# A Strassen-form feed-forward kernel: the next block's chain tiles are loaded into other buffers two products earlier, some transposes stand one product later, and the entry to the second feed-forward is reordered

## Chip, cores and metric

The kernel runs on one core of a Trainium2 chip. The metric is the time of one execution on the device in microseconds (us); several executions are given by their median. The page of the profile and the trace are of one further execution, taken by the hardware profiler.

## The reference, cut to what matters

One layer with the same weights for 256 context tokens and 256 latent tokens, everything in float32, model width 2048, feed-forward width 5632:

```
def half_step_ffn(x, mod, i, g, w_up, w_down):
    h = adaln(x, g, mod, i)                     # RMS norm, scale, shift
    a, b = jnp.split(h @ w_up, 2, axis=-1)
    return x + 0.5 * mod[:, i + 2, None, :] * ((jax.nn.silu(a) * b) @ w_down)

xl = half_step_ffn(xl, mod_l, 0, ...)           # first feed-forward, latent
xc = half_step_ffn(xc, mod_c, 0, ...)           # and context tokens
...                                             # mixing: attention and mLSTM heads
xl = half_step_ffn(xl, mod_l, 6, ...)           # second feed-forward, latent tokens only
return rms_norm(xl, g_final)
```

The modulation vectors (`mod_l`, `mod_c`) are products of a condition vector with a 2048 x 18432 matrix. They are computed beside the feed-forwards.

## The kernel before

**Products.** A float32 product is made of three TensorE products in fp32r. Both operands are split into a high part (ScalarE rounds a copy, `ringhi` on L140 or L170) and a low part (VectorE subtracts, `ringlo` on L141 or L171); high x high, high x low and low x high are added up in PSUM. Weights stream from HBM in tiles of 128 x 2048 float32 (1 MB). Every weight tile is split when it is used, into a ring of four half-tile slots, so that the split of one tile runs while TensorE works on the tile before.

**Blocks.** The hidden width is cut into 11 blocks of 512. In the up-projections of most blocks a 2 x 2 block product is done with seven products instead of eight. `quad(n)` does this for block n. Its table `order` has one row for each of the seven products (`a11`, `a12`, `n1`, `s4`, `s2`, `s3`, `a22`, named by their token form), and each is done in two tiles, q = 0 and 1. So a block has 14 places, 0 to 13: place 2m + q is tile q of product m. The columns of a row are the token form, where the weight tile comes from, the PSUM bank, whether it starts fresh, what is issued behind the split, and what is done with the result.

**The chain.** Four of the seven products take their weight tiles from two buffers, `chain_[0]` and `chain_[1]`: they are loaded with the first weight form (places 0 and 1), and after each use GpSimd issues a DMA that adds the next difference of weights to them in place (`accum`, L784). Places 2 and 3 take plain tiles from the pool `raw` (three buffers), places 6 and 7 take two more raw tiles (`ra`) to which an accumulating DMA adds another form for places 10 and 11. The function `again` behind place 12 + q loads `chain_[q]` for the next block, since before this the tile is still read. These loads stand on the queue of the SP engine, in order, together with all others: `chain` loads on L817 (first feed-forward), L1159 (its down-projection) and L2113 (second feed-forward), plain tiles on L952, `ra` tiles on L947.

**First feed-forward.** `quad(1)` to `quad(10)` do the up-projection; each product has 24 matmuls of 128 x 512 for a tile. Results are combined (`ca`, L896 and L897), transposed on TensorE (L893) and sent to HBM. The loads and vector work of the modulation products (`sraw`, L263 and L292) are woven in. `pair(p)` then does the down-projection of two hidden blocks at a time in the same seven products, with its own `again`.

**Second feed-forward.** It has 256 tokens only. Its entry does the first hidden block in plain products (L1955 to L1962: Silu, multiply, `split_hid`). Then two streams are interleaved: `quads()` (seven blocks in the seven-product form, 12 matmuls for each tile) and `units()` (three blocks in plain form and all down-projections, 24 matmuls for each tile). `places()` says how many units follow each place. `turned()` transposes a finished hidden tile on TensorE (L2049) once at least three tiles have passed since it was made (`turn[0][-1] + 3 > tiles[0]` holds it back), and splits it into `hid2h` and `hid2l` (L2052, L2054). The token forms (`token_forms`, L2000, L2001 and L2005) are made at the entry. PSUM is handed from one set of pools to another there (`banks.close()`), so the first matmul of the second feed-forward proper waits for the last reader of the old banks, the multiply on L1961.

A scheduler orders the instructions of each engine. `tc.keep_in_program_order(ins)` pins an instruction to where it was written.

Of the kernel before, what the change touches and what calls it, by code (L numbers as in the profile page):

```python
# [9 lines left out]
F32 = mybir.dt.float32  # L10
# [4 lines left out]
ALU = mybir.AluOpType  # L15
# [4 lines left out]
P = 128  # L20
# [41 lines left out]
def tile_layer(ctx: ExitStack, tc: tile.TileContext, I: dict, out: bass.AP):  # L62
# [53 lines left out]
    cbT = vecs[:, 272:288]  # L116

    def raw_tile(n=2048):
        t = wp.tile([P, 2048], F32, tag="raw", name="raw", bufs=3)
        return t if n == 2048 else t[:, :n]  # L120
# [16 lines left out]
    def split_whole(raw):  # L137

        hi, lo = ring(2)
        nc.scalar.activation(hi, raw, AF.Copy)  # L140
        nc.vector.tensor_tensor(lo, raw, hi.bitcast(F32), op=ALU.subtract)  # L141
        return lambda w: (hi[:, w], lo[:, w])

    def load_whole(src):
# [640 lines left out]
    with pool(name="f1u", bufs=1) as f1u:  # L785
# [30 lines left out]
        def first_chain(n, c):  # L816
            nc.sync.dma_start(chain_[c], part(n, 0, c))  # L817
# [81 lines left out]
        def quad(n, after=lambda step: None):  # L899
# [36 lines left out]
            def chained(ab, c):  # L936
                return lambda q: accum(chain_[q], part(n, ab, c + q))

            def again(q):
                if n + 1 < NB:  # L940
                    first_chain(n + 1, q)
                else:
                    nc.sync.dma_start(chain_[q], I["w_dn1"][0, 2 * q])

            def loaded(q):
                ra[q] = raw_tile()
                nc.sync.dma_start(ra[q], part(n, 1, 2 + q))  # L947
                return ra[q]

            def plain(q):  # L950
# [155 lines left out]
    def pair(p):  # L1106
# [44 lines left out]

        def loaded(m, cb):
            raw = raw_tile()
            nc.sync.dma_start(raw, w(m, cb))
            return raw

        def again(c):
            if p + 1 < NP:
                nc.sync.dma_start(chain_[c], I["w_dn1"][2 * p + 2, 2 * c])  # L1159

        def b22(c):
            ra[c] = loaded(1, 2 * c + 1)
            return ra[c]
# [7 lines left out]
            ("a11", held, X, True, lambda c: accum(chain_[c], w(0, 2 * c + 1)), c11x),  # L1171
            ("a12", lambda c: loaded(1, 2 * c), Z, True, None, c11z),
# [3 lines left out]
            ("s3", lambda c: ra[c], X, False, None, x3),  # L1176
            ("a22", held, Y, True, again, c21),
        )
# [32 lines left out]
    for p in range(NP):  # L1211
        pair(p)

    def block_products(b, wt, t):
# [707 lines left out]
    with f2x:  # L1922
# [28 lines left out]
        for f in range(NPRE, FB):  # L1951
            pab = []
            for ab in range(2):
                wt = load_split(I["w_up2"][f, ab])
                b = bank()[:, :T]  # L1955
                for k in range(KT):
                    mm3(b, *wt(slice(k * P, (k + 1) * P)), h2hi[:, k, :T], h2lo[:, k, :T], k == 0, k == KT - 1)
                pab.append(b)
            sa = sab_tile()[:, :T]
            nc.scalar.activation(sa, pab[0], AF.Silu)  # L1960
            nc.vector.tensor_tensor(sa, sa, pab[1], op=ALU.mult)  # L1961
            split_hid(hids[0], f, sa)  # L1962
        hscm.__exit__(None, None, None)
# [30 lines left out]

        def ra_tile():
            return f2b.tile([P, 2048], F32, tag="ra", name="ra")

        def token_forms():
# [8 lines left out]

            def difference(v, x, y):
                (h1, l1), (h2, l2) = f32(x), f32(y)
                sub(v, h1, h2)  # L2010
                nc.vector.tensor_tensor(v, v, l1, op=ALU.add)
                sub(v, v, l2)
# [6 lines left out]
            v, w = (acc2[:, t, 1024:].rearrange("p (k c) -> p k c", k=8) for t in range(2))  # L2019
            difference(v, a22, a21)  # L2020
            put(n1, v)
# [15 lines left out]
        def turned():  # L2037

            if not turn or turn[0][-1] + 3 > tiles[0]:
                return  # L2040
# [27 lines left out]
        def quad(n):  # L2068
# [53 lines left out]
            def plain(q):  # L2122
# [290 lines left out]
```

## Time and profile before

| | |
|---|---|
| median of 3 runs | 2645.22 us (2639.3 to 2656.01) |
| profiled execution, own time | 2644.05 us |
| its span, first to last instruction | 2642.3 us |
| granted TensorE clock, mean | 0.996 |
| TensorE (PE) busy | 2595.9 us, 98% |
| weight loads (PEld) busy | 2148.3 us, 81% |
| VectorE (DVE) busy | 2181.9 us, 83% |
| ScalarE (ACT) busy | 1345.2 us, 51% |
| first feed-forward, up | about 150 to 960 us |
| first feed-forward, down | about 960 to 1330 us |
| mixing | about 1330 to 1930 us |
| second feed-forward | about 1930 to 2643 us |

Busy time is the union of an engine's instructions. Idle time of an engine is given with the event that ended it. A number such as 1.79 in square brackets behind an instruction is how long its engine stood idle just before.

### The profile page before, as it was taken

The page shows a single profiled execution, that of the slowest core. Times are in us where ns is not written, and L with a number is a line of the kernel's source. Part 1 is how long each engine was busy: PE and PEld are TensorE (multiplying, and loading weights), DVE is VectorE, ACT ScalarE, POOL GpSimd, SP SyncE. Part 2 cuts the span into 40 slices and gives each one's busy share as a digit, 9 for nine tenths or more (in the row PEclk, how much of TensorE's full clock was granted, in tenths as well). Part 3 has the DMA queues.
Part 4 walks back from the last instruction along what each step waited for, and adds up shares of the span by engine and source line. Part 5 has one row for each costly group of instructions (what it writes and reads, how often), then busy time and mean ns, then how long its engine had stood idle before and what let it go on. Part 6 is the DMA issues. An engine that isn't in the chain of part 4 may idle for free. (4 is left out here: it accounts for less than half of the span.)

```text
span 2642.3 us, 33359 instructions
## 1 busy us (share of the span) xinstructions
PE 2595.9 (98%) x12670; PEld 2148.3 (81%) x12670; DVE 2181.9 (83%) x2817; ACT 1345.2 (51%) x1547; POOL 210.7 (8%) x265
## 2 busy tenths in 40 slices
PE   8999999999999999999999999999999999999998
PEld 5787888888888878888889888877898888888887
DVE  6687888878878778888886979798598888887888
ACT  4354444544444455444454346346476555555554
POOL 0000001100000100010110000111000000000001
PEclk9999999999999999999999999999999999999999
DMA  9979999999999988889985867574568999889886
GB/s 376 343 229 259 257 283 269 271 285 280 271 280 268 276 230 237 221 208 230 231 244 215 315 227 246 207 271 159 175 253 262 294 273 295 259 271 307 285 244 188
DMA packets 136800, 679.94 MB, mean 257 GB/s; under 512 B 14392, under 2 KB 24376, under 8 KB 75840
## 3 DMA queue, kind: packets, MB, share of 16 engines
q1 hardware_dynamic: 108384, 496.92, 50.4%
q0 software_dynamic: 27968, 180.37, 34.8%
q8 instruction: 99, 1.62, 0.2%
q10 hardware_dynamic: 288, 0.52, 0.1%
q14 instruction: 61, 0.50, 0.1%
HBM read 658.82 MB, written 18.94 MB: 256 GB/s over the span
## 5 line engine op out<-in xcount | busy, mean ns | idle before, releaser
L170 ACT ACTIVATE ringhi<-raw 128x1024 fp32r<-128x1024 f32 (+4 forms) x363 | 370.6, 1025 | 429.0 <-PE mm L194 286.3
L171 DVE TENSOR_TENSOR ringlo<-raw,ringhi 128x1024 fp32r<-128x1024 f32 (+3 forms) x340 | 405.7, 1203 | 125.6 <-ACT ringhi L170 110.8
L192 PE MATMUL mm<-ringhi,hhi 128*128 128x512 f32 (+3 forms) x1024 | 391.0, 384 | 0.6 <-ACT ringhi L170 0.6
L193 PE MATMUL mm<-ringlo,hhi 128*128 128x512 f32 (+3 forms) x1024 | 387.5, 378 | 1.0 <-DVE ringlo L171 0.9
L194 PE MATMUL mm<-ringhi,hlo 128*128 128x512 f32 (+3 forms) x1024 | 387.2, 378 | 0.0
L170 ACT ACTIVATE ringhi<-chain 128x1024 fp32r<-128x1024 f32 x240 | 253.1, 1059 | 239.9 <-PE mm L194 143.3
L171 DVE TENSOR_TENSOR ringlo<-chain,ringhi 128x1024 fp32r<-128x1024 f32 x240 | 290.0, 1221 | 69.8 <-ACT ringhi L170 69.0
L263 DVE SCALAR_TENSOR_TENSOR junk<-sraw,cBh 128x1024 fp8e5<-128x1024 f32 x192 | 234.4, 1221 | 44.9 <-DMA sraw<-in_w_mt 42.6
L193 PEld LDWEIGHTS mm<-ringlo,hhi 128*128 128x128 f32 x1024 | 192.7, 188 | 33.5 <-DVE ringlo L171 2.6
L194 PEld LDWEIGHTS mm<-ringhi,hlo 128*128 128x128 f32 x1024 | 192.5, 188 | 33.4
L192 PEld LDWEIGHTS mm<-ringhi,hhi 128*128 128x128 f32 x1024 | 192.5, 188 | 31.7 <-ACT ringhi L170 0.8
L140 ACT ACTIVATE ringhi<-raw 128x2048 fp32r<-128x2048 f32 x78 | 149.7, 1920 | 129.3 <-PE mm L155 75.8
L141 DVE TENSOR_TENSOR ringlo<-raw,ringhi 128x2048 fp32r<-128x2048 f32 x78 | 178.6, 2289 | 39.1 <-ACT ringhi L140 37.6
L141 DVE TENSOR_TENSOR ringlo<-chain,ringhi 128x2048 fp32r<-128x2048 f32 x56 | 128.2, 2288 | 27.6 <-ACT ringhi L140 27.5
L140 ACT ACTIVATE ringhi<-chain 128x2048 fp32r<-128x2048 f32 x56 | 107.5, 1919 | 81.1 <-PE mm L155 26.9
L154 PE MATMUL mm<-ringhi,hid2h 128*128 128x512 f32 x320 | 124.7, 390 | 0.0
L155 PE MATMUL mm<-ringhi,hid2l 128*128 128x512 f32 x320 | 124.5, 389 | 0.0
L784 POOL DMA_DIRECT2D chain<-in_w_up1b x60 | 52.4, 873 | 651.5 <-DVE ringlo L171 543.1
L263 DVE SCALAR_TENSOR_TENSOR sr<-sr,cBl 128x1024 f32<-128x1024 f32 x72 | 87.1, 1215 | 7.2 <-DMA sr<-in_w_mt 7.1
L194 PE MATMUL mm<-hhi,ringlo 128*128 128x512 f32 (+1 forms) x256 | 87.9, 343 | 4.5 <-DVE ringlo L171 4.4
L192 PE MATMUL mm<-hhi,ringhi 128*128 128x512 f32 (+1 forms) x256 | 88.7, 347 | 0.0
L193 PE MATMUL mm<-hlo,ringhi 128*128 128x512 f32 (+1 forms) x256 | 87.0, 340 | 0.0
(513 smaller groups left out, 5940.2 us busy)
## 6 DMA issues: line engine op xcount, KB each, us to landing
raw<-in_w_dn SPq DMA_DIRECT2D x70, 1024.0 KB, 7.5
sraw<-in_w_mt SPq DMA_DIRECT2D x128, 512.0 KB, 7.7
chain<-in_w_up1b POOLq DMA_DIRECT2D x60, 1024.0 KB, 10.9
raw<-in_w_up1b SPq DMA_DIRECT2D x40, 1024.0 KB, 9.3
raw<-in_w_up2b SPq DMA_DIRECT2D x38, 1024.0 KB, 7.6
sr<-in_w_mt SPq DMA_DIRECT2D x69, 512.0 KB, 5.5
mraw<-in_w_m SPq DMA_DIRECT2D x32, 1024.0 KB, 9.2
chain<-in_w_dn POOLq DMA_DIRECT2D x30, 1024.0 KB, 8.5
```

The costliest lines, as they stand in the source:

```text
L140: nc.scalar.activation(hi, raw, AF.Copy)
L141: nc.vector.tensor_tensor(lo, raw, hi.bitcast(F32), op=ALU.subtract)
L154: nc.tensor.matmul(out_ap, sh, mh, start=first, stop=False, skip_group_check=True)
L155: nc.tensor.matmul(out_ap, sl, mh, start=False, stop=False, skip_group_check=True)
L170: nc.scalar.activation(hi, src, AF.Copy)
L171: vector[0].tensor_tensor(lo, src, hi.bitcast(F32), op=ALU.subtract)
L192: tensor[0].matmul(out_ap, sh, mh, start=first, stop=False, skip_group_check=skip)
L193: tensor[0].matmul(out_ap, sh, ml, start=False, stop=False, skip_group_check=skip)
L194: tensor[0].matmul(out_ap, sl, mh, start=False, stop=last, skip_group_check=skip)
L263: ins = nc.vector.scalar_tensor_tensor(junk() if junk else raw, raw, 1.0, cB[s], op0=ALU.mult, op1=ALU.mult, accum_out=mT[:, i, s, kt, h : ...
L784: accum = lambda dst, src: nc.gpsimd.dma_start(dst, src, accum_op=ALU.add)
```

## The change

**Buffers.** In the first feed-forward the three raw tiles become named buffers in a list `free`. `take()` removes the first of the list, `give(t)` puts one back at the end. The chain's two tiles join the rotation: while block n is in place 8 (`s2`, q = 0) the first chain tile of block n + 1 is loaded into a free buffer, in place 10 (`s3`, q = 0) the second (`ahead`); `passed` makes it the chain's tile in places 12 and 13 and gives the old one back. `pair` does the same at `s3` (`next_first`). In the second feed-forward the chain's tiles and the `ra` tiles of the third form (`s4`, `s3`) change places from block to block: the next chain tile is loaded into `ra[q]` behind the split of place 10 + q, and the old chain tile serves as `ra[q]` of the next block.

**Transposes.** A tile of the second token half that carries a minus sign (`turn[0][3] < 0 and turn[0][1]`) is transposed once four tiles have passed, not three.

**Entry of the second feed-forward.** The split of the last hidden tile of block 0 (`split_hid` for f = 3) is written behind the first unit. The first split of a weight tile there, and the first subtraction of the token forms, are pinned in program order.

```
+    free = [wp.tile([P, 2048], F32, name=f"raw{i}", bufs=1) for i in range(3)]
+    def take():
+        return free.pop(0)
+    def give(t):
+        free.append(t)
     def raw_tile(n=2048):
-        t = wp.tile([P, 2048], F32, tag="raw", name="raw", bufs=3)
+        t = take()
+        give(t)
...
# split_whole
+        if in_order:
+            in_order.pop()
+            tc.keep_in_program_order(low)
...
# quad, first feed-forward
-            def again(q):
-                if n + 1 < NB:
-                    first_chain(n + 1, q)
-                else:
-                    nc.sync.dma_start(chain_[q], I["w_dn1"][0, 2 * q])
+            def ahead(q):
+                following[q] = take()
+                nc.sync.dma_start(following[q], part(n + 1, 0, q) if n + 1 < NB else I["w_dn1"][0, 2 * q])
+            def after_s2(q):
+                chained(0, 2)(q)
+                if not q:
+                    ahead(0)
+            def after_s3(q):
+                give(ra[q])
+                if not q:
+                    ahead(1)
+            def passed(q):
+                give(chain_[q])
+                chain_[q] = following[q]
...
-                (s2, held, X, False, chained(0, 2), c12),
-                (s3, lambda q: ra[q], X, False, None, c22),
-                (a22, held, Y, True, again, c21),
+                (s2, held, X, False, after_s2, c12),
+                (s3, lambda q: ra[q], X, False, after_s3, c22),
+                (a22, held, Y, True, passed, c21),
...
# pair, down-projection of the first feed-forward
+        def next_first(c):
             if p + 1 < NP:
-                nc.sync.dma_start(chain_[c], I["w_dn1"][2 * p + 2, 2 * c])
+                following[c] = take()
+                nc.sync.dma_start(following[c], I["w_dn1"][2 * p + 2, 2 * c])
+            give(ra[c])
...
# entry of the second feed-forward
-            split_hid(hids[0], f, sa)
+            if f < FB - 1:
+                split_hid(hids[0], f, sa)
+        in_order.append(True)
...
+                if in_turn:
+                    tc.keep_in_program_order(ins)
...
-            if not turn or turn[0][-1] + 3 > tiles[0]:
+            if not turn or turn[0][-1] + 3 + (turn[0][3] < 0 and turn[0][1]) > tiles[0]:
...
# quad, second feed-forward
-            def again(q):
+            def ahead(q):
                 after = [x for x in QUADS if x > n]
                 if after:
-                    nc.sync.dma_start(chain_[q], part(after[0], 0, q))
+                    nc.sync.dma_start(ra[q], part(after[0], 0, q))
+            def passed(q):
+                spare[q], chain_[q] = chain_[q], ra[q]
             def loaded(q):
-                ra[q] = ra_tile()
+                ra[q] = spare[q]
...
-                (s3, lambda q: ra[q], "X", False, None, c22),
-                (a22, held, "Y", True, again, c21),
+                (s3, lambda q: ra[q], "X", False, ahead, c22),
+                (a22, held, "Y", True, passed, c21),
...
# units, behind the first one
+                if sa is not None:
+                    split_hid(hids[0], FB - 1, sa)
+                    sa = None
```

**The SP queue in the first feed-forward**, toward the end of a block of the up-projection. Before, L952 loads plain tile 1 of the next block, L947 `ra` tile 0 of the next block, and L817 the chain's two tiles of the next block.

```order
L952 DMA raw_3149<-in_w_up1b 128x2048
L947 DMA raw_3259<-in_w_up1b 128x2048
L292 DMA sraw_2871<-in_w_mt 128x1024
L884 DMA hid3_1399<-stg_2894 128x512
L817 DMA chain0_1416<-in_w_up1b 128x2048
L292 DMA sraw_2915<-in_w_mt 128x1024
L292 DMA sraw_2956<-in_w_mt 128x1024
L884 DMA hid3_1399<-stg_2975 128x512
L817 DMA chain1_1417<-in_w_up1b 128x2048
```

In the changed kernel L958 is `ahead` (a chain tile of the next block), L981 a plain tile and L976 an `ra` tile; the buffer's name no longer tells the role.

```order
L958 DMA raw0_84<-in_w_up1b 128x2048
L981 DMA raw1_85<-in_w_up1b 128x2048
L307 DMA sraw_2847<-in_w_mt 128x1024
L899 DMA hid3_1386<-stg_2871 128x512
L981 DMA chain0_1403<-in_w_up1b 128x2048
L307 DMA sraw_2892<-in_w_mt 128x1024
L307 DMA sraw_2932<-in_w_mt 128x1024
L899 DMA hid3_1386<-stg_2951 128x512
L976 DMA chain1_1404<-in_w_up1b 128x2048
```

The sequence of transfers is the same in both, four weight tiles in the same four slots. Only the roles moved: the slots that loaded plain 1, `ra` 0, chain 0 and chain 1 now load chain 1, plain 0, plain 1 and `ra` 0. Chain 0 stands in the slot of a weight tile still further ahead, where plain 0 was.

**TensorE in the second feed-forward**, at the end of a block. Before, the transposes of the block's last hidden tile (L2049) stand behind a down-projection tile and ahead of the first product of the next block (`X`).

```order
L155 MATMUL mm<-ringhi,hid2l 128x512
L160 MATMUL mm<-ringlo,hid2h 128x512 x8
L2049 MATMUL tr<-ident,ca 128x128 x4
L154 MATMUL X<-ringhi,h2hi 128x512
L155 MATMUL X<-ringhi,h2lo 128x512
```

In the changed kernel the same transposes are L2090, behind the first tile of `X` (L169, L170, L175).

```order
L169 MATMUL X<-ringhi,h2hi 128x512
L170 MATMUL X<-ringhi,h2lo 128x512
L175 MATMUL X<-ringlo,h2hi 128x512 x4
L2090 MATMUL tr<-ident,ca 128x128 x4
L169 MATMUL X<-ringhi,h2hi 128x512
```

They moved back by one tile of 12 matmuls. This is so at the end of six of the seven blocks. In two of the six, two groups of transposes of a plain block follow and move back too.

**VectorE at the entry of the second feed-forward.** Before, rows on L2000 and L2011 are parts of the token forms, L141 is the low part of the first weight tile and L1961 the multiply that reads the last of the old PSUM banks.

```order
L2000 TENSOR_TENSOR acc_14841<-h2hi 128x1024
L1945 SCALAR_TENSOR_TENSOR sab<-sab,shift 128x256
L2011 TENSOR_TENSOR acc_14841<-acc_14841,h2lo 128x1024
L1933 TENSOR_TENSOR hid2l<-sab,hid2h 128x256
L2000 TENSOR_TENSOR acc_14841<-acc_14841,h2lo 128x1024 x2
L141 TENSOR_TENSOR ringlo<-raw,ringhi 128x2048
L1961 TENSOR_TENSOR sab<-sab,mm 128x256
```

In the changed kernel the multiply is L1999, the low part L151, and L2039 and L2052 are the token forms.

```order
L2039 TENSOR_TENSOR acc_14688<-acc_14688,h2lo 128x1024
L1983 SCALAR_TENSOR_TENSOR sab<-sab,shift 128x256
L2039 TENSOR_TENSOR s3f<-acc_14688,s3f 128x1024
L1971 TENSOR_TENSOR hid2l<-sab,hid2h 128x256
L1999 TENSOR_TENSOR sab<-sab,mm 128x256
L151 TENSOR_TENSOR ringlo<-raw_86,ringhi 128x2048
L1971 TENSOR_TENSOR hid2l<-sab,hid2h 128x256
L2039 TENSOR_TENSOR acc_14688<-h2hi 128x1024
L151 TENSOR_TENSOR ringlo<-raw_84,ringhi 128x2048
L2052 TENSOR_TENSOR acc_14688<-acc_14688,h2lo 128x1024
L2039 TENSOR_TENSOR acc_14688<-acc_14688,h2lo 128x1024
```

The multiply now stands ahead of the first low part. One of the two differences of the token forms (three operations) moved from ahead of it to behind it, between the low parts, and the low part of `s3f` moved ahead of it.

More of the change, by code (lines that the diff above doesn't have):

```diff
@@ L140, in split_whole @@
         nc.scalar.activation(hi, raw, AF.Copy)
-        nc.vector.tensor_tensor(lo, raw, hi.bitcast(F32), op=ALU.subtract)
+        low = nc.vector.tensor_tensor(lo, raw, hi.bitcast(F32), op=ALU.subtract)
+        if in_order:
+            in_order.pop()
+            tc.keep_in_program_order(low)
         return lambda w: (hi[:, w], lo[:, w])
+    in_order = []
     def load_whole(src):
@@ L1150, in c21, with loaded, passed @@
             through_gate(2 * s + 1, 2 * c)
-        def loaded(m, cb):
-            raw = raw_tile()
+        def loaded(m, cb, raw):
             nc.sync.dma_start(raw, w(m, cb))
             return raw
-        def again(c):
+        following = {}
+        def next_first(c):
             if p + 1 < NP:
-                nc.sync.dma_start(chain_[c], I["w_dn1"][2 * p + 2, 2 * c])
+                following[c] = take()
+                nc.sync.dma_start(following[c], I["w_dn1"][2 * p + 2, 2 * c])
+            give(ra[c])
+        def passed(c):
+            give(chain_[c])
+            chain_[c] = following.get(c)
         def b22(c):
-            ra[c] = loaded(1, 2 * c + 1)
+            ra[c] = loaded(1, 2 * c + 1, take())
             return ra[c]
@@ L1212, in tile_layer @@
         pair(p)
+    free[:] = [t for t in free if any(t is x for x in lasting)]
+    assert len(free) == len(lasting)
     def block_products(b, wt, t):
@@ L1993, in tile_layer @@
         n1, s4, s2, s3 = ([x[:, 0], x[:, 1]] for x in (forms2[g] for g in ("n1", "s4", "s2", "s3")))
-        def ra_tile():
-            return f2b.tile([P, 2048], F32, tag="ra", name="ra")
+        spare = [f2b.tile([P, 2048], F32, name=f"ra{q}", bufs=1) for q in range(2)]
         def token_forms():
@@ L2019, in token_forms @@
             v, w = (acc2[:, t, 1024:].rearrange("p (k c) -> p k c", k=8) for t in range(2))
[L2020 removed]
+            difference(v, a22, a21, True)
             put(n1, v)
```

14 lines of the change are left out of this document (8 added, 6 removed).

## The prediction

> **What bounds the kernel now.** First the page: how much of the span TensorE is busy.
>
> ```profile
> PE 2595.9 (98%) x12670; PEld 2148.3 (81%) x12670; DVE 2181.9 (83%) x2817; ACT 1345.2 (51%) x1547; POOL 210.7 (8%) x265
> ```
>
> TensorE's matmuls fill 98%; no other engine is near. An idle share of 2% may still sit in one stage, so the busy times by stage come next: the first feed-forward up and down, the entry of the second, and the rest of the second.
>
> ```profile
> core 0: us, PE busy (x) PEld busy (x) DVE busy (x) ACT busy (x) POOL busy (x), PEclk, DMA share, GB/s
> 150.00:960.00 810.00, 804.80 (x3609) 663.05 (x3609) 675.23 (x844) 401.04 (x463) 71.54 (x82) 1.00 0.98 272
> 960.00:1330.00 370.00, 367.80 (x1615) 303.65 (x1614) 311.24 (x341) 182.52 (x184) 40.63 (x47) 1.00 0.89 226
> 1982.00:2010.00 28.00, 27.64 (x122) 22.91 (x123) 23.95 (x18) 15.11 (x12) 1.85 (x2) 1.00 0.84 272
> 2010.00:2602.00 592.00, 588.22 (x2631) 485.82 (x2630) 500.84 (x374) 336.93 (x230) 37.19 (x43) 1.00 0.89 274
> ```
>
> In the stages that the change touches TensorE is idle for 810 − 804.80 = 5.2, 2.2, 0.4 and 3.8 us; 1.8 us just ahead of 1982 come to it (below). That is **13.4 us** in all, at full clock, and no edit removes or adds a matmul. So the sum can't be large; the question is which of these gaps go, and whether a new one opens.
>
> Is "busy" at the floor? One run of matmuls in the timeline of TensorE, first and last of thirteen:
>
> ```profile
> 789.76 0.39 PE L194 MATMUL mm<-ringhi,hlo 128*128 128x512 f32 x1
> 792.48 0.39 PE L194 MATMUL mm<-ringhi,hlo 128*128 128x512 f32 x1
> 794.66 0.63 PE L893 MATMUL tr<-ident,ca 128*128 128x128 f32 x4 [1.79 <-DVE ca L897]
> ```
>
> Twelve steps take 2.72 us, 0.227 each; a tile of 24 matmuls takes 5.44 us, one of 12 takes 2.72. The third row is a gap of the kind sought: transposes that wait 1.79 us for a VectorE result.
>
> [...]
>
> **The chain tiles in the first feed-forward.** Who waited for the early loads of L817 (the view of that line):
>
> ```profile
>   ACT ringhi L170: 12.7, 6
> DMA to landing us min/median/max: 4.7/6.5/7.9
> ```
>
> ScalarE stood 12.7 us in six waits. To see what of it reaches TensorE, the two places in time order; SP's issue, ScalarE's wait, VectorE's result, TensorE (for the second, TensorE is above).
>
> ```profile
> 392.81 0.33 SPq L817 DMA_DIRECT2D chain<-in_w_up1b  x1
> 399.88 2.01 ACT L170 ACTIVATE ringhi<-chain 128x1024 fp32r<-128x1024 f32 x2 [1.27 <-DMA chain<-in_w_up1b]
> 404.32 0.50 PE L193 MATMUL mm<-ringlo,hhi 128*128 128x512 f32 x1 [0.90 <-DVE ringlo L171]
> ...
> 783.54 0.34 SPq L817 DMA_DIRECT2D chain<-in_w_up1b  x1
> 791.59 1.06 ACT L170 ACTIVATE ringhi<-chain 128x1024 fp32r<-128x1024 f32 x1 [5.73 <-DMA chain<-in_w_up1b]
> 792.56 0.61 ACT L932 ACTIVATE ca<-ca 128x512 f32<-128x512 f32 x1
> 793.83 0.68 DVE L897 TENSOR_TENSOR ca<-ca,cy 128x512 f32<-128x512 f32 x1
> ```
>
> The load lands 7 to 8 us after its issue; the split of it blocks ScalarE's queue, the Silu behind it (L932) comes late, then VectorE, then TensorE: **0.9 us at 404 and 1.79 us at 794**. The other four waits are swallowed by the ring. The remaining 5.2 − 2.7 = 2.5 us in this stage follow other events (modulation tiles, a store of hidden tiles), and I leave them.
>
> What is late next, once the chain is early? The slots of the SP queue stay, so I set them against the need, ScalarE's first split of each tile in the block that begins at 470.
>
> ```profile
> 452.37 0.33 SPq L952 DMA_DIRECT2D raw<-in_w_up1b  x1
> 457.25 0.33 SPq L947 DMA_DIRECT2D raw<-in_w_up1b  x1
> 462.82 0.33 SPq L817 DMA_DIRECT2D chain<-in_w_up1b  x1
> ...
> 470.52 1.06 ACT L170 ACTIVATE ringhi<-chain 128x1024 fp32r<-128x1024 f32 x1 [0.35 <-PE mm L194]
> 475.98 1.06 ACT L170 ACTIVATE ringhi<-chain 128x1024 fp32r<-128x1024 f32 x1 [3.01 <-PE mm L194]
> 481.89 1.06 ACT L170 ACTIVATE ringhi<-raw 128x1024 fp32r<-128x1024 f32 x1 [0.80 <-PE mm L194]
> 487.35 1.06 ACT L170 ACTIVATE ringhi<-raw 128x1024 fp32r<-128x1024 f32 x1 [0.81 <-PE mm L194]
> ...
> DMA to landing us min/median/max: 7.1/9.3/11.5
> DMA to landing us min/median/max: 6.6/9.3/14.9
> ```
>
> The last two rows are the landing times of the loads on L952 and L947. Before, chain 0 leaves at 462.82 and is needed at 470.52: 7.7 us for a load of 6.5 to 7.9. After, chain 1 leaves at 452.37 for 475.98 (23.6 us), plain 0 at 457.25 for 481.89 (24.6), plain 1 at 462.82 for 487.35 (24.5). The longest load of these lines takes 14.9, so the smallest spare time goes from about zero to some 9 us. Number and size of transfers are the same, hence no more load on the DMA engines. Term: **−2.7 us**, bounds 0 (VectorE, 83% busy here, is late anyway) and −5.2 (all gaps of the stage go).
>
> In `pair` the same swap applies; TensorE's gaps of 2.2 us there mostly follow the stage's first tiles, whose loads are not moved in it. Term 0, bounds 0 and −2.2.
>
> **The end of a block in the second feed-forward.** TensorE's waits there, and one case in time order, ScalarE, VectorE, TensorE:
>
> ```profile
> PE tr L2049 <- DVE ca L2071: 3.8, 4, 1.3
> ...
> 2166.38 1.92 ACT L140 ACTIVATE ringhi<-chain 128x2048 fp32r<-128x2048 f32 x1 [3.41 <-DMA chain<-in_w_up2b]
> 2170.53 0.69 DVE L2071 TENSOR_TENSOR ca<-ca,cy 128x512 f32<-128x512 f32 x1
> 2171.36 0.63 PE L2049 MATMUL tr<-ident,ca 128*128 128x128 f32 x4 [1.29 <-DVE ca L2071]
> ```
>
> Four waits, 3.8 us, the longest 1.3: the whole idle time of the stage. The chain tile again holds back a Silu, and through it the multiply on L2071. The change acts twice: the chain is loaded two places earlier, and the transposes stand 12 matmuls, 2.72 us, later, more than the longest wait. Either is enough for this case. Term: **−3.8 us**, bounds 0 and −3.8.
>
> The transposes that move pull their followers along, ScalarE's and VectorE's splits into `hid2h` and `hid2l`:
>
> ```profile
> 2172.03 0.60 ACT L2052 ACTIVATE hid2h<-tr 128x512 fp32r<-128x512 f32 x1 [1.29 <-PE tr L2049]
> 2174.53 0.68 DVE L2054 SCALAR_TENSOR_TENSOR hid2l<-tr,hid2h 128x512 fp32r<-128x512 f32 x1
> ```
>
> From transposes to the end of `hid2l` it is 2175.21 − 2171.36 = 3.9 us. In the new order 36 matmuls (12 of `X`, 24 of `Y`) stand between the transposes and the first reader of the new hidden tile: 8.2 us. So this is covered, with some 4 us to spare.
>
> **The entry.** VectorE and TensorE around 1980:
>
> ```profile
> 1979.60 2.28 DVE L141 TENSOR_TENSOR ringlo<-raw,ringhi 128x2048 fp32r<-128x2048 f32 x1
> 1981.81 0.41 DVE L1961 TENSOR_TENSOR sab<-sab,mm 128x256 f32<-128x256 f32 x1
> 2001.35 1.22 DVE L2000 TENSOR_TENSOR s4f<-acc,s4f 128x1024 fp32r<-128x1024 f32 x1
> ...
> 1980.26 0.28 PE L194 MATMUL mm<-h2hi,ringlo 128*128 128x256 f32 x1
> 1982.36 0.47 PE L154 MATMUL mm<-ringhi,h2hi 128*128 128x512 f32 x1 [1.82 <-DVE sab L1961]
> ```
>
> The multiply that frees the old banks could begin at 1980.54, when the last matmul ends, but VectorE has just begun a 2.28 us low part and reaches it at 1981.81. With the multiply ahead, TensorE can start at about 1980.6 + 0.41 + 0.1 = 1981.1, 1.2 us earlier. The low part then runs from 1981.0 to 1983.3; a unit reads it after 16 matmuls on the high part, at 1981.1 + 3.6 = 1984.7. In exchange three token operations (1.22 us each, the row of L2000) move behind and one ahead, 2 x 1.22 = 2.4 us more for VectorE by 2010, and TensorE comes 1.2 us sooner: 3.6 us against VectorE's idle 28.00 − 23.95 = 4.05 us. Just covered. Term: **−1.2 us**, bounds +2.3 (the cover fails and one low part is late) and −1.8 (no wait left).
>
> **Sum.** −2.7 − 3.8 − 1.2 = −7.7 us on the profiled execution's own 2644.05 (its span, 2642.3, and 1.75 around it): 2636.3. That execution lies 1.2 us below the median of the runs, 2645.22; I give 2636. The best bound is −13.4 (2630.7). A measurement of this kernel can tell about 1%, 26 us, from no change, so this forecast, 0.3%, lies within it.
>
> **Rivals.**
>
> - **The waits move on to another engine (0.17).** VectorE is 83 to 85% busy in these stages, and a tile made ready early only queues ahead of the same work; each gap comes back somewhere else. Against it: both cases show ScalarE stopped by a landing, with VectorE idle behind it. It would give 2643.
> - **Slower: the hidden forms come late (0.06).** The moved transposes put `hid2h` behind another 1.92 us high part and `hid2l` behind another 2.29 us low part. If the sum passes the 8.2 us, the down-projection waits. The point is 4.3 us more than today's 3.9; the price, one low part of 2.29 us past it at each of six places, +13.7, and the 3.8 still gone: 2644.05 − 7.7 + 13.7 = 2650.
> - **All gaps close (0.04):** −13.4, 2630.7.
> - **Slower still: a load misses its slot (0.02).** If loads took over 24.6 us, each of ten blocks would lose the excess; at 3 us each 2666. The longest seen is 14.9.
> - **The swap has no effect (0.02),** since SP sends the same sequence: 2644. The rows of the order speak against it.
> - **TensorE has hidden room (0.01).** The later chain loads, L1159 and L2113, were waited for by ScalarE as well:
>
> ```profile
>   ACT ringhi L170: 5.4, 2
>   ACT ringhi L140: 13.9, 6
> ```
>
> If all its waits came back whole in the end, 12.7 + 5.4 + 13.9 = 32.0 us, it would be 2612. [...]
>
> **Numbers.** The forecast has 0.68. The range 2628 to 2648 takes in forecast, no effect and all gaps closed, with the scatter of single runs (2639.3 to 2656.01 before). Faster by over 1% needs 26 us where 13.4 are idle: 0.02. Slower by over 1%: 0.03, part of the missed slots and what I don't see. Within 1%: 0.95.
>
> **What would show it.** No wait of ScalarE for the new chain loads in the first feed-forward (12.7 to about 0); no TensorE gap at transposes in either feed-forward for a late Silu; the wait for L2071's successor (L2112) at 0; TensorE's gap at the entry 0.6 us instead of 1.82; idle time of TensorE in 2010 to 2602 under 1 us. I am wrong if the waits for `hid2h` appear ahead of the down-projection, if low parts are late in the first two units and products of the second feed-forward, or if TensorE's idle time stays at 46 us.

## The result, and the profile after

| | before | after |
|---|---|---|
| median | 2645.22 us (13 runs, 2638.21 to 2656.01) | 2635.06 us (13 runs, 2628.88 to 2639.77) |
| profiled execution, own time | 2644.05 us | 2633.05 us |

The medians lie 10.2 us apart. The ratio is 0.9958, 95% interval 0.9946 to 0.997, so the changed kernel takes between 8 and 14 us less. The forecast of 2636 lies 0.9 us above the median after. The change is small and not zero.

TensorE's share of the span, from the page of the changed kernel, and then the four stages as they were shown of before, with the same columns:

```profile
PE 2591.7 (98%) x12670; PEld 2145.9 (82%) x12670; DVE 2180.7 (83%) x2817; ACT 1345.4 (51%) x1547; POOL 210.2 (8%) x265
...
150.00:960.00 810.00, 808.53 (x3635) 666.49 (x3633) 680.71 (x849) 406.73 (x469) 71.39 (x82) 1.00 0.98 273
960.00:1330.00 370.00, 366.56 (x1616) 303.01 (x1615) 311.31 (x344) 180.11 (x180) 42.65 (x49) 1.00 0.90 226
1982.00:2010.00 28.00, 28.00 (x125) 23.21 (x124) 27.40 (x20) 18.27 (x15) 1.85 (x2) 1.00 0.90 261
2010.00:2602.00 592.00, 592.00 (x2650) 489.69 (x2649) 505.75 (x380) 334.64 (x228) 40.46 (x46) 1.00 0.89 277
```

The share is 98% in both, so the page alone would show nothing. By stage TensorE's idle time went from 5.2 to 1.5 us, from 2.2 to 3.4 (the down-projection of the first feed-forward, a little worse), from 0.4 to 0 and from 3.8 to 0. The gap ahead of 1982 is in the waits of TensorE from 1960 to 2602, which have a single row left; the waiters for the multiply ahead of the transposes (L2112, L2071 before) follow it:

```profile
PE mm L169 <- DVE sab L1999: 0.7, 1, 0.7
...
  PEld tr L2090: 0.3, 1
```

1.82 us became 0.7. Together the idle time of these stages fell from 13.4 to 5.6 us: 7.8, beside a forecast sum of 7.7. The span fell by 11.0. The rest is time in which TensorE was busy but slow. From the first to the last matmul on the form `n1` it is 722.4 us before (L192, from 180.7 to 903.1) and 716.7 after (L207, from 180.5 to 897.2): 5.7 less, where the idle time of the stage fell by 3.7. The granted clock (the last column but two of the rows by stage) shows two slow stretches in the profile of before, each behind 1.9 us of idle time. The clock first, then the gaps, with ScalarE's wait ahead of the first:

```profile
212.42:215.83 3.41, 3.41 (x10) 2.67 (x9) 3.38 (x5) 0.91 (x1) 0.59 (x1) 0.50 0.84 126
970.18:973.59 3.41, 3.41 (x9) 2.63 (x8) 3.41 (x5) 0.00 (x0) 0.00 (x0) 0.50 0.78 279
...
208.95 0.60 ACT L918 ACTIVATE c<-mm 128x512 f32<-128x512 f32 x1 [6.55 <-DMA hid<-c]
...
210.54 0.50 PE L192 MATMUL mm<-ringhi,s2h 128*128 128x512 f32 x1 [1.14 <-ACT ringhi L170]
211.80 0.50 PE L193 MATMUL mm<-ringlo,s2h 128*128 128x512 f32 x1 [0.76 <-DVE ringlo L171]
...
968.68 0.50 PE L193 MATMUL tr<-ringlo,hidl 128*128 128x512 f32 x1 [1.90 <-DVE ringlo L171]
```

From 970.19 to 973.18 seven steps take 2.99 us, 0.427 each, beside the 0.227 at a granted clock of 1.00. An estimate by the granted clock of 0.50: 3.41 us held the work of 1.71, so each stretch cost about 1.7 us. With the 7.8 us of idle time that is 11.2, beside the 11.0 of the span. The profile of the changed kernel has no such stretch in the stages that the change touches.

The place at 794 of before, ScalarE and then TensorE, now stands at 784 to 788:

```profile
784.14 1.06 ACT L185 ACTIVATE ringhi<-chain 128x1024 fp32r<-128x1024 f32 x1 [2.96 <-DMA raw<-in_w_up1b]
785.11 0.61 ACT L947 ACTIVATE ca<-ca 128x512 f32<-128x512 f32 x1
...
788.02 0.60 PE L908 MATMUL tr<-ident,ca 128*128 128x128 f32 x4
788.38 0.49 PE L207 MATMUL mm<-ringhi,hhi 128*128 128x512 f32 x1
```

The transposes carry no bracket: TensorE waits for nothing. ScalarE still stands 2.96 us ahead of the chain tile's split. The tile's own load is not the cause: it left at 759.66 and had landed 10.35 us later. Nor is the load that is named there, on L976: it left at 779.05 and landed at 786.79, when the split had long begun. The wait is as long as the ring's ordinary wait at this place (3.01 for the matmul on L194, at 475.98 in the prediction's rows), and I take it for that one.

ScalarE's waits for loads in 150 to 960, and the landing times of the new chain loads (L958):

```profile
ACT ringhi L185 <- DMA raw<-in_w_up1b: 12.3, 4, 4.5
...
DMA to landing us min/median/max: 7.9/10.4/12.2
```

No instruction is recorded as waiting for L958. The 12.3 us have the same size as the 12.7 that went, but they are other waits: beside the 2.96 above they are three in the last block, for accumulating transfers of GpSimd that landed after 17.3 to 20.3 us. The second profile of this kernel has these three too (4.2, 2.9 and 4.4 us); the two of the kernel before have one wait there, of 2.9 and 3.8 us. TensorE has no gap at any of the three.

### The profile page after: what moved, and what is told of

Read it like the earlier page. It is cut to its first block, busy times and chain, and to the rows that moved or that the text cites. A ratio compares the mean times of both kernels' runs of the same rounds, so it can differ in the third digit from the quotient of the medians.

```text
span 2631.3 us, 33355 instructions
## 1 busy us (share of the span) xinstructions
PE 2591.7 (98%) x12670; PEld 2145.9 (82%) x12670; DVE 2180.7 (83%) x2817; ACT 1345.4 (51%) x1547; POOL 210.2 (8%) x265
## 5 line engine op out<-in xcount | busy, mean ns | idle before, releaser
L185 ACT ACTIVATE ringhi<-raw 128x1024 fp32r<-128x1024 f32 (+4 forms) x433 | 444.4, 1030 | 497.9 <-PE mm L209 327.8
L186 DVE TENSOR_TENSOR ringlo<-raw,ringhi 128x1024 fp32r<-128x1024 f32 (+3 forms) x410 | 490.8, 1208 | 145.7 <-ACT ringhi L185 131.8
L207 PE MATMUL mm<-ringhi,hhi 128*128 128x512 f32 (+3 forms) x1024 | 390.9, 384 | 0.6 <-ACT ringhi L185 0.6
L185 ACT ACTIVATE ringhi<-chain 128x1024 fp32r<-128x1024 f32 x170 | 179.7, 1060 | 164.1 <-PE mm L209 117.2
L186 DVE TENSOR_TENSOR ringlo<-chain,ringhi 128x1024 fp32r<-128x1024 f32 x170 | 205.5, 1222 | 47.1 <-ACT ringhi L185 45.6
L207 PEld LDWEIGHTS mm<-ringhi,hhi 128*128 128x128 f32 x1024 | 192.4, 188 | 31.8 <-ACT ringhi L185 0.8
L151 DVE TENSOR_TENSOR ringlo<-raw,ringhi 128x2048 fp32r<-128x2048 f32 x78 | 178.6, 2290 | 39.7 <-ACT ringhi L150 39.6
L169 PE MATMUL mm<-ringhi,hid2h 128*128 128x512 f32 x320 | 124.7, 390 | 0.0
L170 PE MATMUL mm<-ringhi,hid2l 128*128 128x512 f32 x320 | 124.5, 389 | 0.0
L150 ACT ACTIVATE ringhi<-chain 128x2048 fp32r<-128x2048 f32 x44 | 84.5, 1920 | 63.8 <-PE mm L170 27.2
L151 DVE TENSOR_TENSOR ringlo<-chain,ringhi 128x2048 fp32r<-128x2048 f32 x44 | 100.7, 2288 | 13.3 <-ACT ringhi L150 13.3
L150 ACT ACTIVATE ringhi<-ra 128x2048 fp32r<-128x2048 f32 x40 | 76.8, 1921 | 59.6 <-PE Y L170 25.8
L151 DVE TENSOR_TENSOR ringlo<-ra,ringhi 128x2048 fp32r<-128x2048 f32 x40 | 91.5, 2288 | 9.8 <-ACT ringhi L150 9.8
L207 PE MATMUL mm<-hhi,ringhi 128*128 128x512 f32 (+1 forms) x256 | 88.7, 346 | 0.0
```

What stands on the lines that cost most here:

```text
L151: low = nc.vector.tensor_tensor(lo, raw, hi.bitcast(F32), op=ALU.subtract)
L169: nc.tensor.matmul(out_ap, sh, mh, start=first, stop=False, skip_group_check=True)
L170: nc.tensor.matmul(out_ap, sl, mh, start=False, stop=False, skip_group_check=True)
L185: nc.scalar.activation(hi, src, AF.Copy)
L186: vector[0].tensor_tensor(lo, src, hi.bitcast(F32), op=ALU.subtract)
L207: tensor[0].matmul(out_ap, sh, mh, start=first, stop=False, skip_group_check=skip)
```

## Experiments

In the first feed-forward the question was how much the early chain load is worth; in the second, which of the two edits cured the transposes, and how late they may come. Theory A is that of the prediction: a load that lands late stops ScalarE, a Silu behind it is late, then VectorE, then TensorE. Its main rivals are that the waits only move on, and that the gaps are scatter of one execution. The first four kernels shared one set of runs of the kernel before (2645.01 us), the next four another, on another chip (2643.19).

**The first feed-forward put back.** The chain's loads of both projections stand behind places 12 and 13 again.

```
-                (a22, held, Y, True, passed, c21),
+                (a22, held, Y, True, ahead, c21),   # ahead(q) loads chain_[q] itself
```

> The changed kernel, but with the chain loads of the first feed-forward (up and down) behind places 12 and 13 again, into the chain's own buffers; everything in the second feed-forward stays changed. Theory A (the loads were late, ScalarE's queue stopped and TensorE felt it): ScalarE waits again 10 to 16 us for chain loads, TensorE gets back one to three gaps of 0.5 to 2 us in 150 to 960, in all about 3 us, time about 3 us above the changed kernel, 2638. Rival B (DMA scatter from run to run, the loads had nothing to do with it): gaps in 150 to 960 as in the changed kernel, time equal to it. If the 1.9 us gap at 210 us of the kernel before comes back too, it hangs on the loads; if not, it was scatter of one store.

Measured: 2639.21 us median of 12 runs, ratio to before 0.9989 (0.9968 to 1.001). TensorE's waits, ScalarE's waits for the chain, and the longest gap:

```profile
PE tr L908 <- DVE ca L912: 3.9, 3, 2.8
...
ACT ringhi L185 <- DMA chain<-in_w_up1b: 17.1, 7, 6.8
...
794.48 0.63 PE L908 MATMUL tr<-ident,ca 128*128 128x128 f32 x4 [2.84 <-DVE ca L912]
```

The wait near 794 is back at 2.84 us, with two smaller ones at transposes and with ScalarE's waits for the chain. The gap at 210 us of before does not come. This part is worth about 4 us by the medians (2639.2 against 2635.1), but the intervals of the two ratios still overlap, if barely. The trace bears it out: from the first matmul on `hhi` (L207; L192 before) to the first on `sumshh`, the up-projection takes 813.3 us here, 808.9 in the changed kernel and 816.8 in the one before.

**Chain loads later than they ever were**: in the up-projection both behind place 13, otherwise as in the kernel above.

```
-                (a22, held, Y, True, passed, c21),
+                (a22, held, Y, True, lambda q: [ahead(x) for x in range(2 * q)], c21),
```

> The changed kernel with the chain loads of the first feed-forward's up-projection both behind place 13, so that chain tile 0 leaves a tile of 5.4 us later than in the kernel before and the two loads run together. Theory A: ScalarE waits some 5 us in each of the ten blocks, 40 to 60 us in all, of which the ring of two tiles swallows 3 to 4 us each time, as at 794 us in the kernel before (5.7 us of ScalarE cost TensorE 1.8); TensorE gets 1 to 2 us more idle time a block, the kernel is 10 to 20 us above the changed one. Rival B (TensorE does not depend on these loads): under 4 us.

Measured: 2638.8 us median of 12 runs, ratio 0.9973 (0.9959 to 0.9988): no slower than the kernel above, a miss for the theory's size. By the medians it is 3.7 us above the changed kernel, where the theory said 10 to 20 and the rival under 4.

```profile
PE tr L908 <- DVE ca L912: 4.5, 3, 2.3
PE mm L208 <- DVE ringlo L186: 1.5, 2, 0.9
...
ACT ringhi L185 <- DMA chain<-in_w_up1b: 24.3, 10, 6.3
```

ScalarE waits 24.3 us, ten times; TensorE 6.0, five times. Of these, 4.5 us stand at transposes; ahead of the one of 2.33 us a Silu (at 794.08) was queued behind a split that had waited 6.26 us. TensorE shows five waits beside ScalarE's ten, so I read the others as ended while it still had half-tiles of the ring to work on. So the time falls where the rival put it, but TensorE does depend on these loads: the mechanism stands, and the price of a late load was too high.

**Both kernels once more, unchanged.** Each gap in the first profile might have been that execution's own.

> The kernel before, unchanged, one more profiled execution. Question: which of TensorE's gaps in the first feed-forward belong to the order of the work, and which to one execution. Theory A (order): the gaps of 0.90 us at 404 and 1.79 us at 794, which end on a result that waited for the chain's load, come again at the same places, within 1 us of their size; the gap at 210 us with the 7 slow matmuls behind it, which follows one store of hidden tiles that landed after 17.54 us, does not. TensorE is idle 3 to 7 us in 150 to 960, and four waits of 3 to 5 us stand at the transposes of the second feed-forward. Rival B (scatter): the gaps at 404 and 794 stand elsewhere or are missing, and the idle time of 150 to 960 is under 2.5 us; then the part of the gain in the first feed-forward isn't the change's. Time 2640 to 2650.

> The changed kernel, unchanged, one more profiled execution. Theory A: no gap at 404 or 794, TensorE idle 0.5 to 3 us in 150 to 960, none in 2010 to 2602, 0.7 us ahead of 1982 at the entry; what idle time is left in the first feed-forward stands at other places than in the first profile of this kernel. Rival B (scatter): 3 us or more idle in 150 to 960, as in the profile before. Time 2631 to 2640.

Measured: 2643.04 and 2633.49 us. The first feed-forward of the kernel before, then of the changed one; the waits of TensorE there, before and after:

```profile
150.00:960.00 810.00, 805.15 (x3611) 663.38 (x3610) 676.74 (x844) 402.24 (x464) 71.42 (x82) 1.00 0.98 271
...
PE tr L893 <- DVE ca L897: 2.6, 2, 2.5
PE mm L193 <- DVE ringlo L171: 2.1, 3, 1.1
```

```profile
150.00:960.00 810.00, 808.41 (x3633) 665.96 (x3632) 680.18 (x849) 405.17 (x469) 71.40 (x82) 1.00 0.98 273
...
PE mm L208 <- DVE ringlo L186: 1.4, 3, 0.7
```

Idle: 4.9 and 1.6 us, beside 5.2 and 1.5 in the first pair. The amount repeats, but not every place. The gap at the transposes near 790 comes again, at 2.46 us; the one at 404, 0.90 us in the first profile, does not: in its stead are 0.54 at 425, 0.45 at 431 and 1.09 at 901, each before a `ringlo` result. The gap at 210 us of before does not come again either. In the second feed-forward the four waits at the transposes do come again, with 4.2 us in all and 1.4 the longest. So of the two places on which the prediction's 2.7 us rested, one comes every time and the other only in some executions: the kernel with both loads behind place 13 has 0.87 us at 404, the one with the loads put back has none there. Over all twelve profiles, the first feed-forward has waits of TensorE at its transposes in the four with late chain loads (1.8, 2.6, 3.9 and 4.5 us) and in none of the eight with early ones.

The gap near 790, with TensorE's granted clock (the last column but two) in the 3.4 us behind it:

```profile
788.09 0.63 PE L893 MATMUL tr<-ident,ca 128*128 128x128 f32 x4 [2.46 <-DVE ca L897]
...
789.37 0.63 PE L192 MATMUL mm<-ringhi,hhi 128*128 128x512 f32 x1
789.79 0.63 PE L193 MATMUL mm<-ringlo,hhi 128*128 128x512 f32 x1
...
792.35 0.47 PE L193 MATMUL mm<-ringlo,hhi 128*128 128x512 f32 x1
...
789.00:792.40 3.40, 3.40 (x10) 2.60 (x9) 3.37 (x5) 1.75 (x3) 0.89 (x1) 0.52 1.04 213
```

From 789.37 to 792.35 seven steps take 2.98 us, 0.426 each and not 0.227. With the slower step ahead of them that is 1.5 us more, so the gap cost 4.0 us and not 2.46. The same happened at the two places of before that were shown with the result.

**The second feed-forward put back**, buffers and transposes both.

```
-            if not turn or turn[0][-1] + 3 + (turn[0][3] < 0 and turn[0][1]) > tiles[0]:
+            if not turn or turn[0][-1] + 3 > tiles[0]:
...
-                (s3, lambda q: ra[q], "X", False, ahead, c22),
-                (a22, held, "Y", True, passed, c21),
+                (s3, lambda q: ra[q], "X", False, None, c22),
+                (a22, held, "Y", True, ahead, c21),
...
# ahead
-                    nc.sync.dma_start(ra[q], part(after[0], 0, q))
+                    nc.sync.dma_start(chain_[q], part(after[0], 0, q))
```

> The changed kernel, but in the second feed-forward with the chain loaded behind places 12 and 13 again and the transposes after three tiles again. Theory A: TensorE's waits for the multiply ahead of the transposes come back, 3 to 5 waits, 3 to 4 us in all, idle time in the stage again about 3.8 us, time about 4 us above the changed kernel, 2639. Rival B: another wait takes their place already in the changed kernel, so that the time does not move.

Measured: 2638.13 us median of 12 runs, ratio 0.9975 (0.996 to 0.999).

```profile
PE tr L2090 <- DVE ca L2112: 4.5, 5, 1.2
...
ACT ringhi L150 <- DMA chain<-in_w_up2b: 12.8, 6, 3.3
```

The waits of before are back, five and 4.5 us in all. Worth about 3 us by the medians, where the intervals of the two ratios overlap, and 4.5 by the trace.

**One edit of the two at a time.** First the buffers alone put back, so that the chain comes late and the transposes stand one tile later; then the transposes alone put back, so that the chain comes early and they stand where they were. The edits are the two halves of the one above.

> The changed kernel, but in the second feed-forward with the chain loaded behind places 12 and 13 again; the transposes stay one tile of 12 matmuls later. Theory A (either part alone cures these waits): ScalarE waits again 10 to 14 us for chain loads there, but TensorE does not wait for the multiply ahead of the transposes, since 2.7 us of matmuls stand between; idle time of the stage under 1 us, time as the changed kernel. Rival B (only the early load cures them): the waits of 3 to 4 us come back.

> The changed kernel, but with the transposes after three tiles as before; the chain's tiles stay early. Theory A (either part alone): no wait of ScalarE for chain loads, the multiply comes 2 to 4 us earlier, and at least three of the four waits ahead of the transposes are gone, under 1 us left. Rival B (only the later place cures them, since VectorE is late by itself): waits of 3 us or more remain. In the kernel before, the wait at 2338 us followed a ScalarE idle that ended with a VectorE result, not with a landing, so one wait of up to 0.8 us may stay.

Measured: 2632.33 us (5 runs), ratio 0.9955 (0.994 to 0.9971); and 2632.17 us (6 runs), ratio 0.9949 (0.993 to 0.9969). With the chain late, ScalarE's and TensorE's waits:

```profile
ACT ringhi L150 <- DMA chain<-in_w_up2b: 13.6, 6, 3.5
...
PE mm L169 <- ACT ringhi L150: 2.0, 2, 1.5
```

With the chain early, TensorE in 2010 to 2602:

```profile
2010.00:2602.00 592.00, 592.00 (x2650) 489.64 (x2649) 505.54 (x375) 341.17 (x234) 36.95 (x42) 1.00 0.90 276
```

Either edit takes every wait at the transposes away. The earlier load takes all idle time with it; the later transposes leave ScalarE's 13.6 us of waits standing, and in that execution 2.0 us of TensorE's came in at weight tiles, where under 1 was expected. One of these two follows a wait of 5.8 us for a plain tile, so I don't put both down to the chain. In time the two kernels can't be told from the changed one.

The profile of the second of these has a gap that has nothing to do with its edit, the longest of all, in the first feed-forward; its own time is 2645.66 us. TensorE, and VectorE ahead of it:

```profile
439.63 0.79 PE L208 MATMUL mm<-ringlo,s4h 128*128 128x512 f32 x1 [6.83 <-DVE ringlo L186]
...
435.94 1.22 DVE L278 SCALAR_TENSOR_TENSOR junk<-sraw,cBh 128x1024 fp8e5<-128x1024 f32 x1 [11.51 <-DMA sraw<-in_w_mt]
```

VectorE stood 11.51 us for a load of the modulation's weights, with the low part of a weight tile behind it in its queue. It is the prediction's mechanism with other names, and this change does not touch it.

**Transposes later still**, by one more tile and by three more.

```
-  turn[0][-1] + 3 + (turn[0][3] < 0 and turn[0][1]) > tiles[0]
+  turn[0][-1] + 3 + 2 * (turn[0][3] < 0 and turn[0][1]) > tiles[0]    # 4 * in the second kernel
```

> The changed kernel with the transposes held back by one tile more (five instead of four), so that 24 matmuls, 5.4 us, stand between them and the first reader of the hidden tile where the down-projection of the same block follows at once (three of the blocks). The split into hid2h and hid2l took 3.9 us from the transposes in the kernel before. Theory: still covered, idle time of the stage under 1 us, time as the changed kernel. Rival (the hidden forms are the next late thing): waits ahead of the down-projection, 1 us or more each.

> The changed kernel with the transposes held back by three tiles more, so that no matmul stands between them and the down-projection of the same block in three blocks. Theory: TensorE waits there for hid2h, hid2l, or both, up to 3.9 us each, less what it can do on the high part first: 4 to 12 us in all, time 4 to 12 us above the changed kernel. Rival (the forms are made faster than thought, ScalarE and VectorE go ahead of their other work): under 2 us.

Measured: 2634.89 us (7 runs), ratio 0.9967 (0.995 to 0.9985); and 2634.06 us (5 runs), ratio 0.9958 (0.9944 to 0.9972). TensorE's idle time in 2010 to 2602 is 0.0 in both. With three tiles more the loss that the prediction's slower rival priced should have come, and it did not. One place of that kernel, TensorE, then ScalarE and VectorE:

```profile
2257.07 0.60 PE L2090 MATMUL tr<-ident,ca 128*128 128x128 f32 x4
2257.42 0.49 PE L169 MATMUL mm<-ringhi,hid2h 128*128 128x512 f32 x1
...
2259.36 0.39 PE L169 MATMUL mm<-ringhi,hid2h 128*128 128x512 f32 x1
2259.59 0.85 PE L175 MATMUL mm<-ringlo,hid2h 128*128 128x512 f32 x3
2260.28 0.49 PE L170 MATMUL mm<-ringhi,hid2l 128*128 128x512 f32 x1
...
2258.18 0.57 ACT L2093 ACTIVATE hid2h<-tr 128x512 fp32r<-128x512 f32 x1
...
2259.54 0.68 DVE L2095 SCALAR_TENSOR_TENSOR hid2l<-tr,hid2h 128x512 fp32r<-128x512 f32 x1
```

The down-projection begins right behind the transposes. Its first eight matmuls, from 2257.42, belong to the first token half, which was transposed much earlier; the new high form is first read by the ninth, at 2259.36, and is ready at 2258.75. Then the scheduler has put three products of the low weight part ahead of the first reader of the new low form. That starts at 2260.28, and the form is ready at 2260.22. The cover holds by 0.06 us. Three tiles are 36 matmuls, 8.2 us, so this is about what the changed kernel has to spare, not 4.3.

**The entry put back.**

```
-            if f < FB - 1:
-                split_hid(hids[0], f, sa)
-        in_order.append(True)
+            split_hid(hids[0], f, sa)
...
-            difference(v, a22, a21, True)
+            difference(v, a22, a21)
```

> The changed kernel with the old entry to the second feed-forward: all four hidden tiles split in place, nothing pinned there. Theory A: TensorE waits 1.8 us again for the multiply that frees the old banks, against 0.7, so about 1.1 us above the changed kernel; too little for the clock time to show, so the trace decides. Rival B (VectorE's extra 2.4 us come late in the first places, so that the gap was only moved): TensorE's gaps in 1975 to 2045 are equal in sum.

Measured: 2634.31 us median of 8 runs, ratio 0.9963 (0.9949 to 0.9978): no different from the changed kernel in time. The trace tells them apart, by the wait ahead of the first matmul:

```profile
PE mm L169 <- DVE sab L1999: 3.2, 1, 3.2
```

3.2 us against 0.7. In the kernel before this wait was 1.82 in one execution and 2.9 in the other, so in idle time the edit is worth 1.1 to 2.5 us. Idle time is not all of it: at the wait of 3.2 us the granted clock is 0.50 for 6.83 us, of which TensorE idles 1.04.

```profile
1976.01:1982.84 6.83, 5.79 (x14) 4.56 (x15) 6.83 (x8) 1.56 (x2) 0.00 (x0) 0.50 0.93 339
```

Counted by TensorE's starts, the 140 steps from its 9661st instruction on (1965.8 us in the first profile of before) take 19.8 us in all nine executions with the new entry, 20.9 and 24.7 in the two of before, and 25.0 here. So the edit is worth 1.1 to 5.2 us. Behind the wait of 1.82 us the granted clock was 1.00, and the steps took 20.9 us. The medians can't show this, since the interval of each ratio reaches 3 to 4 us to either side. Which part of the edit does it, the later split or the two pins, was not tried.

## Why the prediction was right

- **The cap.** TensorE's gaps in the touched stages were taken as the whole of what could be won, 13.4 us. The span fell by 11.0. But the cap was set too low: that busy time is at the floor was read from thirteen matmuls at full clock, and the same profile has the two stretches at a granted clock of 0.50, by the estimate above 3.4 us more to win.
- **Chain tiles in the first feed-forward, −2.7.** The mechanism is shown: with the late load put back, the waits of ScalarE and the gap at the transposes return. The size is low. In the four executions with late chain loads (before twice, and the two kernels that move them back) TensorE idled 4.6 to 6.0 us in 150 to 960; in the eight with early ones 1.5 to 3.3, but for the one of 9.4. Leaving that one out, the means differ by about 3.1 us of idle time, and by TensorE's starts (the stretch of 816.8 us above) by about 4. The step that failed in part is the choice of places: the gap at 404 comes only in some executions. What made up for it is that 794 costs more than its idle time, up to 4.0 us with the slow matmuls behind it. All gaps were priced at full clock, and behind this one the granted clock was 0.52 in the second profile of before (1.00 in the first).
- **`pair`, 0.** Idle time 2.2 to 3.4 in one pair of profiles, 2.2 to 2.9 in the other: nothing won. The microsecond lost in the first pair is not the change's by what the other runs show: from TensorE's 4701st to its 6361st instruction, a stretch that holds `pair`, it is 376.6 to 377.0 us in the four executions with the old loads and 376.3 to 378.1 in the eight with the new ones.
- **End of a block in the second feed-forward, −3.8.** Idle time 3.8 to 0.0. "Either is enough" held for the waits at the transposes in both kernels that tried it.
- **Hidden forms, covered.** Right in outcome, wrong in the working: the down-projection's first matmul was taken for a reader of the new half, so the cover was set too short, and the rival's price of 2.29 us at six places is not borne out even with transposes three tiles later.
- **Entry, −1.2.** 1.82 to 0.7 in the first profile, −1.1. In the second pair it is −2.2 of idle time and −4.9 by TensorE's starts, outside the bound of −1.8, which left slow matmuls out. The prediction gave 0.6 for what stays. The feared late low parts of the first units show no wait.
- **The sum.** −7.7 forecast, −7.8 of idle time seen, −11.0 in the span. That the first two agree is in part luck: the idle time of the up-projection fell by 3.7 where 2.7 was forecast, but 1.9 of this is the gap in two pieces at 210, which no later profile has and which was not among the terms, and `pair` went the other way by 1.2. The rest of the span is about what the two slow stretches cost. The prediction also said that a measurement tells about 1% from no change. With 13 runs of each kernel the interval is 0.24% wide, and the change stands clear of zero.
- **The rivals.** Waits did move on, but to engines that had room: ScalarE's 12.3 us, most of them in the last block, reach TensorE nowhere. A load that misses its slot costs less than forecast: with the chain as late as it will go, about 4 us and not tens.

## What to carry to other kernels

With TensorE busy for 98%, there was the idle time of the touched stages to win, 13.4 us, and the slow matmuls behind part of it, 0.427 us a step and not 0.227, so the granted clock belongs in the sum. The chain behind each gap (transfer, split, Silu, multiply, transposes) says which edit closes it. A wait of a feeding engine is not to be counted in full: with both loads behind place 13, 24 us of ScalarE's waits came with 6 of TensorE's. Gaps of about a microsecond should be seen in two executions before a term is put on their places; their sum was steadier than the places.

## What the runs showed of the hardware

- **Idle time of 1.9 us cost about 3.6 at two places, and a gap of 2.33 us no more than itself at a third.** In the two profiles that were shown with the result, from 100 us on to 30 us before the end, the record of the granted clock has four stretches at 0.50, of 3.41 us each: from 212.42, 970.18 and 1642.60 before, and from 1636.82 after. In the 3.41 us ahead of them TensorE idled 1.90, 1.90, 2.29 and 2.29 us. Those of before begin 222 and 197 times 3.413 us apart. Cut at that spacing, no other window of the two profiles has over 1.82 us of idle time, and behind each of them the granted clock is 1.00. The length of a gap alone does not tell the cases apart: one of 1.86 us, which ends at 962.19 in the profile after, has 1.00 behind it, and so has the one of 2.33 us with both loads behind place 13. Below, a window with 1.86 us idle and 0.50 behind it (the kernel with the second feed-forward put back), and the window in which the gap of 2.33 ends, with 1.85 us idle and 1.00 behind it. Where a matmul ends is modelled in these traces, so these figures are approximate. Why the clock falls was not shown.

```profile
960.45:963.86 3.41, 1.55 (x8) 0.96 (x7) 3.41 (x4) 3.41 (x4) 0.00 (x0) 1.00 0.12 50
963.86:967.27 3.41, 3.41 (x10) 2.67 (x9) 3.37 (x4) 0.43 (x1) 0.00 (x0) 0.50 0.52 163
...
794.33:797.74 3.41, 1.56 (x9) 1.41 (x10) 3.41 (x5) 2.38 (x4) 0.00 (x0) 1.00 0.87 247
797.74:801.15 3.41, 3.41 (x17) 2.80 (x16) 3.38 (x7) 2.17 (x3) 0.89 (x1) 1.00 0.90 135
```

- **One store landed after 17.54 us in one execution and after 7.07 in another.** In the profile of before a store of hidden tiles, issued at 191.33, landed after 17.54 us; ScalarE waited 6.55 us for it, and the gap at 210 came behind. In the profile after, the same store, issued at 191.14, took 7.07. In another execution (the transposes alone put back) a load of modulation weights held VectorE for 11.51 us and TensorE behind it for 6.83, and 3.4 us at a granted clock of 0.50 followed. With the 1.7 us estimated for a stretch at 0.50, the first cost about 3.6 us and the second over 8, beside the 10.2 between the medians. Why they are late stays open.
